# Attention's seven products: signs turned so that weight sums are additions, two of the sums made by accumulating transfers, the second product ahead of the sixth

## The chip, the cores and the metric

One core of one Trainium2 chip runs the whole program. The metric is device time in microseconds (us) of one execution, the median of several. Five engines matter: PE (matrix products, with PEld for its weight loads), DVE (elementwise work), ACT (copies, exponentials, scaled copies), POOL (copies, and the queue of transfers that can add to what lies at their goal), SP (the queue of plain loads).

## The reference

A model of two layers on 512 tokens of width 1024. Layer one is attention with three groups of heads (windows 128, 512, 2048 at dilations 1, 4, 16), then a gated feed-forward part; layer two is an mLSTM mixer and a second feed-forward part. The change lies in the projections of the attention:

```python
proj = (xn @ w_in).reshape(B, S, N_GROUPS, 3, ATTN_HEADS, ATTN_HEAD_DIM)   # w_in: 1024 x 9216
for g, (window, dilation) in enumerate(DIL_CONFIGS):
    q = apply_partial_rope(proj[:, :, g, 0], positions) * scale
    k = apply_partial_rope(proj[:, :, g, 1], positions)
    v = proj[:, :, g, 2]
    o, lse = dilated_window_attention(q, k, v, window, dilation)
    ...
```

All is float32. A product is made of three matmuls on split operands: each operand is a high part (rounded to the format that PE multiplies) and a low part (the rest), and high by high, high by low, low by high are added.

## The kernel before, in words

**Units.** Heads are taken in four pairs (`pr` 0 to 3) and three groups (`g` 0 to 2). A unit `a<pr>g<g>` makes q and k of two heads in one group: two blocks of 256 columns of `w_in`, for 512 tokens. In eleven units (all but `a0g0`) this 2 x 2 block product (weights halved by rows into W1., W2. and by q and k into W.1, W.2; tokens halved) is done with seven products instead of eight, by Winograd's form of Strassen's method. `QK_ORDER` holds the order of the products. Each is 24 matmuls of 128x256 (`qk_unit`, L1100).

**Weights of a unit.** `load_part` (L969) puts the load of one quarter, W11, W12, W22 or W21 (512 KB), on SP's queue. `prepare_part` makes the weight operand of one product. Sums are made in place by DVE (L979):

- P5: W11 becomes W12 - W11
- P6: W11 becomes W22 - that
- P7: W12 becomes W22 - W12
- P4: W21 becomes W21 - W11 (by now P6's operand); made once P2, which uses the plain W21, has been split, in unit a1g2 with P7

Then `split_chunk` makes the high part on ACT (L239) and the low part on DVE (L241). After P2 the next unit's W11 is loaded into the place of this one's, after P7 its W12, after P3 and P4 its W22 and W21. `Feed` prepares two to four products ahead of the one that PE works on.

**Banks of a unit.** P1 goes to bank C11. ACT copies C11 to bank U (L1078, `fill_u`). P2 adds to C11, which is then q of the first half of tokens. P6 adds to U, and ACT copies U to `vu[:, 1]` (L1041). P7 adds to U; DVE adds `vu[:, 0]` (P5's bank, copied by L1038), and this is k of the second half. P3 adds to P5's bank, DVE adds `vu[:, 1]`: k of the first half. P4 adds to U: q of the second half. P7 and P3 end in L1061, P2 and P4 in L1021 (`pack`) and L1055.

**Token sums.** `sum_of` makes S1 to S4 from four blocks of the normalized input (L1272) once, and they serve all units.

**Values.** Two more units, `v0` and `v1` (`values_phase`), make the values of some groups by the same seven products, with sums by DVE (`prepare_values`, L1319); there the order already has P2 ahead of P6.

**Order of the work.** The scores, exponentials and values of the pair before run between the products. `defer` and `advance` place them by ticks: a tick passes after the products at places 1, 3, 5 and 6 (from 0) of a unit in pairs 1 to 3. `run` keeps a block of matmuls together. On POOL's queue lie the copies of the rope's result (L649, L644), stores of the transposed exponentials to DRAM (L897) and loads of them (L902) that wait for those stores. When the program is built, a scheduler puts the instructions of every engine in one order, by their place in the program and by when it expects their operands; on the chip each engine keeps to that order. `behind_scores`, `behind_factors` and `tc.issue_after` give it further constraints.

Accumulating transfers of other parts of the kernel, from which the prediction takes rows: `f1T` (feed-forward output weights, from DRAM, L1887), `oraws` (mLSTM output weights, from DRAM, L2406), `f0T1l` (from SBUF, L1602).

Of the kernel before, what the change touches and what calls it, by code (L numbers as in the profile page):

```python
# [14 lines left out]
AF = mybir.ActivationFunctionType  # L15
ALU = mybir.AluOpType
AX = mybir.AxisListType
P = 128
# [58 lines left out]
def tile_hybrid_dilated_attn_mlstm(  # L77
# [350 lines left out]
    with ExitStack() as actx:  # L428
# [517 lines left out]
        behind_u = []  # L946
        postponed, behind_seventh, held_maxima, copied, differences = [], [], [], [None], [None, None]

        QK_ORDER = ("P1", "P5", "P6", "P2", "P7", "P3", "P4")
        four_k = lambda t: t.rearrange("p (k n) -> p k n", k=4)  # L950
        parts_of = {}

        def by_products(pr, g):
            return g > 0 or pr >= PRODUCTS_FROM

        def load_part(pr, g, key):
            if g > 2:
                pr, g = pr + 1, 0
            if pr == HEADS // 2:
                return  # L960
            if (pr, g, key) == (1, 0, "W11"):
                t = ap.tile([P, 1024], F32, tag="rot", name="a1g0W11")
            elif pr == 0 and key == "W11":
                t = place(("w1", "s1")[g - 1], "a0g%dW11" % g, (P, 1024))
            else:
                pool_, tag, bufs = (ap2, "wa", 1) if key == "W11" else (wp, "wraw", W_BUFS)
                t = pool_.tile([P, 1024], F32, tag=tag, name="a%dg%d%s" % (pr, g, key), bufs=bufs)
            k0, c0 = (int(key[1]) - 1) * 4 * P, g * 3 * D + (int(key[2]) - 1) * D + pr * 256
            nc.sync.dma_start(four_k(t), w_in[k0:k0 + 4 * P, c0:c0 + 256].rearrange("(k p) n -> p k n", p=P))  # L969
            parts_of.setdefault((pr, g), {})[key] = t  # L970

        sixth = [None]
# [1 line left out]
        def prepare_part(pr, g, name):  # L974
            b = parts_of[pr, g]

            def less(out, x, y):
                with behind_scores():
                    nc.vector.tensor_tensor(b[out], b[x], b[y], op=ALU.subtract)  # L979
            src = {"P1": "W11", "P5": "W11", "P6": "W11", "P2": "W21", "P7": "W12", "P3": "W22", "P4": "W21"}[name]  # L980
            if name == "P5":
                less("W11", "W12", "W11")
                differences[0] = last_on(DVE)
            elif name == "P6":
                less("W11", "W22", "W11")
            elif name == "P7":
                with tc.issue_after(sixth[0]) if (pr, g) in ((1, 2), (2, 0)) else nullcontext():
                    less("W12", "W22", "W12")
            with tc.issue_after(differences[1]) if pr and g and name == "P2" else nullcontext():
                whl = split_chunk((b[src], 1024, four_k, "a%dg%d%s" % (pr, g, name)), NARROW)  # L990
            if name == "P6":
                differences[1] = last_on(ACT)
                if (pr, g) in ((1, 2), (2, 0)):
                    sixth[0] = last_on(DVE)
            if (pr, g, name) == (1, 2, "P7"):
                with tc.issue_after(last_on(DVE)):
                    less("W21", "W21", "W11")
            if name == "P5" and not late[0]:
                sixth[0] = last_on(DVE)
            follows = g < 2 or (pr and by_products(pr + 1, 0))  # L1000
            if name == "P2":
                if (pr, g) != (1, 2):
                    less("W21", "W21", "W11")
                if follows:
                    load_part(pr, g + 1, "W11")
            elif name == "P7" and follows:
                load_part(pr, g + 1, "W12")
            elif name in ("P3", "P4") and follows:
                load_part(pr, g + 1, src)
            return whl  # L1010

        def qk_unit(pr, g, qk, then=None):
# [4 lines left out]
            acc = {}  # L1017
            rot = vu = None

            def pack(q, src):  # L1020
                nc.scalar.activation(two_m(rot[0][quarter(q)]), src, AF.Copy)  # L1021

            def each(out, src, th, fn):

# [8 lines left out]
            def finish(name):  # L1033
                nonlocal rot, vu
                if name == "P5":
                    vu = ap.tile([P, 2, SEQ], F32, tag="vu", name=nm + "vu")
                    with behind_factors() if g == 0 else nullcontext():
                        nc.scalar.activation(vu[:, 0], acc["p5"], AF.Copy)  # L1038
                    ahead_of_casts[0] = last_on(ACT)
                elif name == "P6":  # L1040
                    nc.scalar.activation(vu[:, 1], acc["u"], AF.Copy)  # L1041
                    ahead_of_casts[0] = last_on(ACT)
                    if g == 1:
                        copied[0] = last_on(ACT)
                elif name in ("P2", "P4"):
                    th = int(name == "P4")
                    src = acc[target[name]]
                    if th == 0:
                        if g == 0:
                            rot = [npl.tile([P, SEQ], F32, tag=tag, name="rot") for tag in ("rbc", "ssum")]  # L1050
                        else:
                            t = ap.tile([P, 2, SEQ], F32, tag="rot", name="rot")
                            rot = t[:, 0], t[:, 1]
                    pack(th, two_m(src[:R]))
                    each(qk[0], [src], th, lambda to, x: nc.scalar.activation(to, x, AF.Copy))  # L1055
                    ahead_of_casts[0] = last_on(ACT)
                elif name in ("P7", "P3"):
                    th = int(name == "P7")
                    with behind_scores():
                        each(qk[1], [acc[target[name]], vu[:, 1 - th]], th,  # L1060
                             lambda to, x, y: nc.vector.tensor_tensor(to, x, y, op=ALU.add))  # L1061
                    if g == 2:
                        ahead_of_splits[0] = last_on(DVE)
                    if g:
                        pack(2 + th, halves(qk[1], th)[:R])
                    else:
                        for m in range(2):
                            nc.scalar.activation(packed(rot, 2 + th, m, True), turned(qk, 2 + th, m, True), AF.Copy)
                    if g == 2:
                        ahead_of_casts[0] = last_on(ACT)  # L1070
# [191 lines left out]
        def sum_of(name):  # L1262
            nonlocal heads_s
            if name == "S1":
                heads_s = ap.tile([P, 4, 4, HALF], F32R, tag="heads", name="S12")
                sums["chain"] = place("w4", "Sr", (P, 4, HALF))
            raw = place("w5", "S3r", (P, 4, HALF)) if name == "S3" else sums["chain"]
            of = lambda t, kh: lambda i, ks: xblock(t, kh, i)
            chain = lambda i, ks: raw[:, ks]
            x, y, op = {"S1": (of(1, 0), of(1, 1), ALU.add), "S2": (chain, of(0, 0), ALU.subtract),  # L1270
                        "S3": (of(0, 0), of(1, 0), ALU.subtract), "S4": (of(0, 1), chain, ALU.subtract)}[name]
            two(lambda i, ks: nc.vector.tensor_tensor(raw[:, ks], x(i, ks), y(i, ks), op=op))  # L1272
            split_sum(name, raw)

        def first_values():
# [39 lines left out]
        def prepare_values(u, name, hf):  # L1315
            b = {key: t for (key, i), t in blocks[u].items() if i == hf}

            def less(out, x, y):
                nc.vector.tensor_tensor(b[out], b[x], b[y], op=ALU.subtract)  # L1319
            src = {"P1": "W11", "P5": "W11", "P6": "W11", "P2": "W21", "P7": "W12", "P3": "W22", "P4": "W21"}[name]  # L1320
            if name == "P5":
                less("W11", "W12", "W11")
            elif name == "P6":
                less("W11", "W22", "W11")
            elif name == "P7":
                less("W12", "W22", "W12")
            elif name == "P4":
                less("W21", "W21", "W11")
            whl = split_chunk((b[src], 1024, two_k, "v%d%s_%d" % (u, name, hf)))
            following = {"P1": "W11", "P7": "W12", "P3": "W22", "P4": "W21"}.get(name)  # L1330
            if following is not None:
                load_block(u + 1, following, hf)
            if u == len(UNITS) - 1 and hf == 1:
                for key in {"P2": ("W11",), "P6": ("W12", "W22"), "P3": ("W21",)}.get(name, ()):
                    load_part(1, 0, key)
            return whl
# [9 lines left out]
        def values_phase():  # L1346
# [8 lines left out]

            def add(to, src):
                for m in range(2):
                    nc.vector.tensor_tensor(to[:, m], src[m], to[:, m], op=ALU.add)

            def stored(u, tile_, half, n):  # L1360
                nc.gpsimd.dma_start(vD[UNITS[u][n]][half * HALF:(half + 1) * HALF].rearrange("(m p) f -> p m f", p=P), tile_)
# [1466 lines left out]
```

## Time and profile before

| what | value |
|---|---|
| median of three runs | 1342.1 us (1341.83 to 1342.5) |
| profiled execution | 1342.11 us, span of the program in it 1340.3 us |
| granted TensorE clock | 0.999 |
| 57 to 400 us: PE idle, as the list of waits gives it | 4.1 us in nine waits |
| products of the seven-product units | 24 matmuls, 0.11 us from start to start |
| a sum of a quarter on DVE (L979) | 1.2 to 1.3 us, 44 of them |
| high part on ACT, low part on DVE | 1.05 us, 1.22 us |

A row of the timeline has start, duration, engine, line, operation, what it writes and from what, shapes and count; in brackets the idle time before it and what ended it. A row of the list of waits reads: who, for whom, total us, times, longest. A group has its count, busy us, mean ns of one, and the idle time before. In names, `a2g2u` is bank U of unit a2g2, `c` and `p` its banks C11 and P5, `a2g2W` its quarters of weights, `a2g2P_h` and `P_l` a product's high and low part, `S`, `S3`, `S4` the token sums, `xa` the input. `PEld` is a weight load. A landing is counted from issue to arrival.

### The profile page before, as it was taken

To read this page: it belongs to the slowest core of one execution; us is meant where nothing else is said; L and a number is where in the kernel's file an instruction comes from. 1 tells how busy PE (TensorE), PEld (TensorE's weight loads), DVE (VectorE), ACT (ScalarE), POOL (GpSimd) and SP (SyncE) were. 2 spreads that over 40 slices of the span, in tenths; PEclk is the share of its full clock that TensorE was granted. 3 is DMA by queue.
4 is the path that set the end of the run, shared out by engine and by line. 5 is a ranking of instruction groups with operands and counts; after the bars stand their busy time and mean duration, and the time that the engine had idled before them with its cause. 6 is when DMAs were issued, how large, how long until landed. Compare 5 with 4: busy or idle time off the path is not lost. (4 is left out here: it accounts for less than half of the span.)

```text
span 1340.3 us, 23696 instructions
## 1 busy us (share of the span) xinstructions
PE 1323.3 (99%) x9244; PEld 1221.1 (91%) x9244; DVE 1146.4 (86%) x1804; ACT 823.1 (61%) x1313; POOL 214.7 (16%) x292
## 2 busy tenths in 40 slices
PE   9999999999999999999999999999999999999997
PEld 7898899999998889999999998888897999999886
DVE  7988789898876399888888899898889988987887
ACT  6676577677674355554587464795565655559855
POOL 3000014141412001000010110123330211112113
PEclk9999999999999999999999999999999999999999
DMA  9354244556586357334362743326684635447864
GB/s 306 128 181 155 82 142 137 178 152 191 158 288 200 131 146 178 108 110 127 126 161 77 173 138 94 103 64 173 132 168 131 155 108 166 142 142 176 185 173 103
DMA packets 146809, 200.71 MB, mean 150 GB/s; under 512 B 9316, under 2 KB 111524, under 8 KB 146696
## 3 DMA queue, kind: packets, MB, share of 16 engines
q1 hardware_dynamic: 120128, 140.73, 33.4%
q0 software_dynamic: 25344, 58.25, 18.9%
q8 instruction: 73, 1.20, 0.4%
q10 hardware_dynamic: 1224, 0.21, 0.1%
q14 instruction: 40, 0.33, 0.1%
HBM read 172.02 MB, written 22.54 MB: 145 GB/s over the span
## 5 line engine op out<-in xcount | busy, mean ns | idle before, releaser
L1863 POOL DMA_DIRECT2D f0S<-in_ffn_w_out_dram x10 | 8.8, 876 | 246.7 <-DVE f0hid L1782 162.6
L2617 POOL DMA_DIRECT2D hD<-hB x32 | 20.8, 656 | 111.2 <-DVE hB L2614 111.1
L1887 POOL DMA_DIRECT2D f1T<-in_ffn_w_out_dram x15 | 17.8, 1185 | 86.6 <-ACT f1T L1890 26.1
L276 PE MATMUL mo<-n_h,mo_k_h 128*128 128x512 f32 x64 | 25.4, 396 | 0.0
L276 PE MATMUL f1j<-n_h,f1j_l 128*128 128x512 f32 x64 | 25.1, 392 | 0.2 <-DVE f1j_l L241 0.2
L276 PE MATMUL mo<-n_l,mo_k_h 128*128 128x512 f32 x64 | 25.2, 394 | 0.0
L276 PE MATMUL mo<-n_h,mo_k_l 128*128 128x512 f32 x64 | 25.2, 393 | 0.0
L276 PE MATMUL awo<-ao_h,awo_k_h 128*128 128x512 f32 x64 | 25.2, 393 | 0.0
L276 PE MATMUL mqk<-n_h,mqk_k_h 128*128 128x512 f32 x64 | 25.1, 392 | 0.0
L276 PE MATMUL mqk<-n_l,mqk_k_h 128*128 128x512 f32 x64 | 25.1, 392 | 0.0
L276 PE MATMUL f0j<-n_h,f0j_h 128*128 128x512 f32 x64 | 25.0, 391 | 0.0
L276 PE MATMUL f1j<-n_h,f1j_h 128*128 128x512 f32 x64 | 25.0, 391 | 0.0
L276 PE MATMUL awo<-ao_h,awo_k_l 128*128 128x512 f32 x64 | 25.0, 391 | 0.0
L276 PE MATMUL mqk<-n_h,mqk_k_l 128*128 128x512 f32 x64 | 25.0, 390 | 0.0
L241 DVE TENSOR_TENSOR v1P_l<-v1W,v1P_h 128x1024 fp32r<-128x1024 f32 x14 | 17.1, 1223 | 9.2 <-ACT v1P_h L239 9.1
L276 PE MATMUL awo<-ao_l,awo_k_h 128*128 128x512 f32 x64 | 25.0, 390 | 0.0
L276 PE MATMUL f1j<-n_l,f1j_h 128*128 128x512 f32 x64 | 24.9, 390 | 0.0
L276 PE MATMUL f0j<-n_h,f0j_l 128*128 128x512 f32 x64 | 24.9, 390 | 0.0
L276 PE MATMUL f0j<-n_l,f0j_h 128*128 128x512 f32 x64 | 24.9, 389 | 0.0
L241 DVE TENSOR_TENSOR v0P_l<-v0W,v0P_h 128x1024 fp32r<-128x1024 f32 x14 | 17.0, 1221 | 6.9 <-ACT v0P_h L239 6.9
L239 ACT ACTIVATE v1P_h<-v1W 128x1024 fp32r<-128x1024 f32 x14 | 14.8, 1058 | 12.8 <-PE v1u L1398 4.0
L1890 ACT ACTIVATE f1T<-f1T 128x1024 f32<-128x1024 f32 x15 | 15.8, 1053 | 8.9 <-DVE f1P_2w_l L241 3.1
(2812 smaller groups left out, 6106.4 us busy)
## 6 DMA issues: line engine op xcount, KB each, us to landing
f0j_w<-in_ffn_w_in_dram SPq DMA_DIRECT2D x17, 512.0 KB, 5.3
f1j_w<-in_ffn_w_in_dram SPq DMA_DIRECT2D x17, 512.0 KB, 6.7
f1T<-in_ffn_w_out_dram POOLq DMA_DIRECT2D x15, 512.0 KB, 6.7
f0hid<-in_ffn_w_in_dram SPq DMA_DIRECT2D x9, 512.0 KB, 5.2
f1hid<-in_ffn_w_in_dram SPq DMA_DIRECT2D x9, 512.0 KB, 5.3
v0W<-in_attn_w_in_dram SPq DMA_DIRECT2D x8, 512.0 KB, 6.2
v1W<-in_attn_w_in_dram SPq DMA_DIRECT2D x8, 512.0 KB, 4.0
awo_k_w<-in_attn_w_out_dram SPq DMA_DIRECT2D x8, 512.0 KB, 4.2
```

Source lines behind the costliest of these rows:

```text
L239: nc.scalar.activation(hi[:, :n], raw[:, :n], AF.Copy)
L241: nc.vector.tensor_tensor(lo[:, :n], raw[:, :n], hi[:, :n].bitcast(F32), op=ALU.subtract)
L276: nc.tensor.matmul(acc, whl[a][:, k, m * P:(m + 1) * P], pairs[b][kk], start=(kk == 0 and (a, b) == SPLITS[0]), stop=(kk == nk - 1 and (a, ...
L1863: nc.gpsimd.dma_start(t, src[1][:, ks], accum_op=ALU.add)
L1887: nc.gpsimd.dma_start(view(to), weight_rows(hk * UNITS + u, n), accum_op=ALU.add)
L1890: nc.scalar.activation(x, x, AF.Copy, scale=-1.0)
L2617: nc.gpsimd.dma_start(hD[k // 4].rearrange("(b i) x -> i b x", i=R)[:, :, c0:c0 + R], t[R * a_:R * (a_ + 1)])
```

## The change

The signs of the method are turned so that every sum of weights is an addition; the token sums S1, S2, S4 and the results change sign to make up for it (a scale of -1 in ACT's copies of q, `scalar_tensor_tensor` with -1 where DVE subtracted or added).

In the eleven units of q and k:

- P5's and P6's sums stay on DVE, as additions.
- P7's sum is made by a transfer on POOL's queue, issued with P5: W12 (no longer needed plain once P5's sum has read it) gets W22 added from DRAM.
- P4's sum is made by a transfer on POOL's queue, issued with P6: W21 gets W11 added, SBUF to SBUF. It has to wait for P6's sum and for P2's split.
- P2 is done ahead of P6. P6's split is to follow P2's on ACT (before: P2's followed P6's).
- The next unit's W11 is loaded after P6, and has to wait until P4's transfer has read this one's.
- Two constraints on P7's difference in units a1g2 and a2g0 fall away.

In the value units the sums stay on DVE.

```diff
-        QK_ORDER = ("P1", "P5", "P6", "P2", "P7", "P3", "P4")
+        QK_ORDER = ("P1", "P5", "P2", "P6", "P7", "P3", "P4")
...
+        def weights_part(pr, g, key):
+            k0, c0 = (int(key[1]) - 1) * 4 * P, g * 3 * D + (int(key[2]) - 1) * D + pr * 256
+            return w_in[k0:k0 + 4 * P, c0:c0 + 256].rearrange("(k p) n -> p k n", p=P)
...
-            def less(out, x, y):
+            def total(out, x, y):
                 with behind_scores():
-                    nc.vector.tensor_tensor(b[out], b[x], b[y], op=ALU.subtract)
+                    nc.vector.tensor_tensor(b[out], b[x], b[y], op=ALU.add)
             src = {"P1": "W11", "P5": "W11", "P6": "W11", "P2": "W21", "P7": "W12", "P3": "W22", "P4": "W21"}[name]
             if name == "P5":
-                less("W11", "W12", "W11")
+                total("W11", "W12", "W11")
                 differences[0] = last_on(DVE)
+                nc.gpsimd.dma_start(four_k(b["W12"]), weights_part(pr, g, "W22"), accum_op=ALU.add)
             elif name == "P6":
-                less("W11", "W22", "W11")
-            elif name == "P7":
-                with tc.issue_after(sixth[0]) if (pr, g) in ((1, 2), (2, 0)) else nullcontext():
-                    less("W12", "W22", "W12")
-            with tc.issue_after(differences[1]) if pr and g and name == "P2" else nullcontext():
+                total("W11", "W22", "W11")
+            with tc.issue_after(differences[1]) if pr and g and name == "P6" else nullcontext():
                 whl = split_chunk((b[src], 1024, four_k, "a%dg%d%s" % (pr, g, name)), NARROW)
-            if name == "P6":
+            if name == "P2":
                 differences[1] = last_on(ACT)
                 if (pr, g) in ((1, 2), (2, 0)):
                     sixth[0] = last_on(DVE)
-            if (pr, g, name) == (1, 2, "P7"):
-                with tc.issue_after(last_on(DVE)):
-                    less("W21", "W21", "W11")
+            if name == "P6":
+                nc.gpsimd.dma_start(b["W21"], b["W11"], accum_op=ALU.add)
...
-            if name == "P2":
-                if (pr, g) != (1, 2):
-                    less("W21", "W21", "W11")
+            if name == "P6":
                 if follows:
                     load_part(pr, g + 1, "W11")
...
-            def pack(q, src):
-                nc.scalar.activation(two_m(rot[0][quarter(q)]), src, AF.Copy)
+            def pack(q, src, scale=1.0):
+                nc.scalar.activation(two_m(rot[0][quarter(q)]), src, AF.Copy, scale=scale)
...
-                    pack(th, two_m(src[:R]))
-                    each(qk[0], [src], th, lambda to, x: nc.scalar.activation(to, x, AF.Copy))
+                    pack(th, two_m(src[:R]), -1.0)
+                    each(qk[0], [src], th, lambda to, x: nc.scalar.activation(to, x, AF.Copy, scale=-1.0))
...
-            x, y, op = {"S1": (of(1, 0), of(1, 1), ALU.add), "S2": (chain, of(0, 0), ALU.subtract),
-                        "S3": (of(0, 0), of(1, 0), ALU.subtract), "S4": (of(0, 1), chain, ALU.subtract)}[name]
-            two(lambda i, ks: nc.vector.tensor_tensor(raw[:, ks], x(i, ks), y(i, ks), op=op))
+            x, y, both = {"S1": (of(1, 1), of(1, 0), False), "S2": (chain, of(0, 0), True),
+                          "S3": (of(0, 0), of(1, 0), False), "S4": (of(0, 1), chain, True)}[name]
...
+                if both:
+                    nc.vector.scalar_tensor_tensor(raw[:, ks], x(i, ks), -1.0, y(i, ks), op0=ALU.mult, op1=ALU.subtract)
...
-                    nc.vector.tensor_tensor(to[:, m], src[m], to[:, m], op=ALU.add)
+                    nc.vector.scalar_tensor_tensor(to[:, m], src[m], -1.0, to[:, m], op0=ALU.mult, op1=ALU.subtract)
```

More of the change, by code (lines that the diff above doesn't have):

```diff
@@ L967, in load_part @@
                 t = pool_.tile([P, 1024], F32, tag=tag, name="a%dg%d%s" % (pr, g, key), bufs=bufs)
-            k0, c0 = (int(key[1]) - 1) * 4 * P, g * 3 * D + (int(key[2]) - 1) * D + pr * 256
-            nc.sync.dma_start(four_k(t), w_in[k0:k0 + 4 * P, c0:c0 + 256].rearrange("(k p) n -> p k n", p=P))
+            nc.sync.dma_start(four_k(t), weights_part(pr, g, key))
             parts_of.setdefault((pr, g), {})[key] = t
@@ L1269, in sum_of, with combine @@
             chain = lambda i, ks: raw[:, ks]
-            x, y, op = {"S1": (of(1, 0), of(1, 1), ALU.add), "S2": (chain, of(0, 0), ALU.subtract),
-                        "S3": (of(0, 0), of(1, 0), ALU.subtract), "S4": (of(0, 1), chain, ALU.subtract)}[name]
-            two(lambda i, ks: nc.vector.tensor_tensor(raw[:, ks], x(i, ks), y(i, ks), op=op))
+            x, y, both = {"S1": (of(1, 1), of(1, 0), False), "S2": (chain, of(0, 0), True),
+                          "S3": (of(0, 0), of(1, 0), False), "S4": (of(0, 1), chain, True)}[name]
+            def combine(i, ks):
+                if both:
+                    nc.vector.scalar_tensor_tensor(raw[:, ks], x(i, ks), -1.0, y(i, ks), op0=ALU.mult, op1=ALU.subtract)
+                else:
+                    nc.vector.tensor_tensor(raw[:, ks], x(i, ks), y(i, ks), op=ALU.subtract)
+            two(combine)
             split_sum(name, raw)
@@ L1316, in prepare_values, with total @@
             b = {key: t for (key, i), t in blocks[u].items() if i == hf}
-            def less(out, x, y):
-                nc.vector.tensor_tensor(b[out], b[x], b[y], op=ALU.subtract)
+            def total(out, x, y):
+                nc.vector.tensor_tensor(b[out], b[x], b[y], op=ALU.add)
             src = {"P1": "W11", "P5": "W11", "P6": "W11", "P2": "W21", "P7": "W12", "P3": "W22", "P4": "W21"}[name]
             if name == "P5":
-                less("W11", "W12", "W11")
+                total("W11", "W12", "W11")
             elif name == "P6":
-                less("W11", "W22", "W11")
+                total("W11", "W22", "W11")
             elif name == "P7":
-                less("W12", "W22", "W12")
+                total("W12", "W22", "W12")
             elif name == "P4":
-                less("W21", "W21", "W11")
+                total("W21", "W21", "W11")
             whl = split_chunk((b[src], 1024, two_k, "v%d%s_%d" % (u, name, hf)))
```

## The prediction

> **What bounds the kernel now.** I read the page first, then who waited for whom on PE in the stretch that the change touches (57 to 400 us), then PE's rows in order of time around the longest wait.
>
> ```profile
> PE 1323.3 (99%) x9244; PEld 1221.1 (91%) x9244; DVE 1146.4 (86%) x1804; ACT 823.1 (61%) x1313; POOL 214.7 (16%) x292
> ```
>
> PE is busy for 1323.3 us of a span of 1340.3. The change keeps every matmul, so what it can give is PE's waiting in the seven-product units. The list of waits shows how little that is:
>
> ```profile
> PE a1g2u L1100 <- DVE a1g2P_l L241: 1.3, 1, 1.3
> PE a2g2u L1100 <- DVE a2g2P_l L241: 0.6, 1, 0.6
> PE a3g2u L1100 <- DVE a3g2P_l L241: 0.5, 1, 0.5
> ...
> PE a1g2c L1100 <- ACT a1g2P_h L239: 0.3, 1, 0.3
> PE a0g1u L1100 <- DVE a0g1P_l L241: 0.3, 1, 0.3
> PE a0g2u L1100 <- DVE a0g2P_l L241: 0.3, 1, 0.3
> ```
>
> Six waits, 3.3 us together: five for the low part of a weight half (DVE, L241), one for a high part. All are in P6 or P2 but a0g1's, which is in P7. PE loses more than the idle time, since a matmul's modelled end runs past the next one's start. The worst place, unit a1g2:
>
> ```profile
> 223.76 0.28 PE L1100 MATMUL a1g2p<-S,a1g2P_l 128*128 128x256 f32 x1
> 223.87 0.39 PE L1100 MATMUL a1g2u<-S,a1g2P_h 128*128 128x256 f32 x2
> 224.60 0.38 PE L1100 MATMUL a1g2c<-xa_h,a1g2P_h 128*128 128x256 f32 x1 [0.34 <-ACT a1g2P_h L239]
> 224.83 0.28 PE L1100 MATMUL a1g2c<-xa_l,a1g2P_h 128*128 128x256 f32 x1
> 226.37 0.39 PE L1100 MATMUL a1g2u<-S,a1g2P_l 128*128 128x256 f32 x1 [1.27 <-DVE a1g2P_l L241]
> 226.60 0.40 PE L1100 MATMUL a1g2u<-S,a1g2P_h 128*128 128x256 f32 x2
> ```
>
> Undisturbed, matmuls start 0.11 us apart (223.76, 223.87). Here 224.83 is followed by 226.37 and that by 226.60: 1.43 + 0.12 = 1.55 us lost where 1.27 are listed, 0.28 on top of the wait. So the six cost 3.3 + 6 x 0.28 = 5.0 us, 0.37% of the run: the ceiling of the gain. The rows show a second thing: two matmuls of P2 (a1g2c) stand inside P6 (a1g2u). PE's queue is not in the order of the products; work that was expected to be ready had been put ahead.
>
> **The change part by part.**
>
> *Two of four sums leave DVE.* Eleven units with four sums each; the costliest and the cheapest group:
>
> ```profile
> L979 DVE TENSOR_TENSOR a1g2W<-a1g2W,a1g2W 128x1024 f32<-128x1024 f32 x4 | 5.3, 1320 | 0.0
> L979 DVE TENSOR_TENSOR a0g1W<-a0g1W,a0g1W 128x1024 f32<-128x1024 f32 x4 | 4.8, 1209 | 0.0
> ```
>
> 22 instructions at 1.2 to 1.3 us are 27 us of DVE, none of it on PE's path by itself: it counts where a low part is queued behind a sum.
>
> *P2 ahead of P6.* P2 needs no sum, and P6's split gets 24 matmuls x 0.11 = 2.7 us more, beyond any of these waits. Only in a1g2 does more stand before it: the rope on DVE, from the shuffle to the last addition.
>
> ```profile
> 222.38 0.75 DVE L630 STREAM_SHUFFLE rot<-rot 128x512 f32<-128x512 f32 x1
> 224.49 0.69 DVE L639 TENSOR_TENSOR rot<-rot 128x512 f32<-128x512 f32 x1
> ```
>
> With P2's low part (1.2 us) put ahead of the rope, the rope ends at 225.2 + 1.2 = 226.4 and P6's low part at 227.6; P6's third matmul is then due at 224.1 + 2.7 = 226.8. Between 0 (low part ahead of the rope) and 0.8 us I take 0.4. a0g1's P7 now has its sum from a transfer begun two products earlier than its subtraction was. Back come 5.0 - 0.4 = 4.6 us.
>
> *P7 directly behind P6.* Both add into the bank U, which L1041 copies in between. Until now P2 stood there. The last matmul of P6, and the copy:
>
> ```profile
> 207.44 0.28 PE L1100 MATMUL a1g1u<-S,a1g1P_l 128*128 128x256 f32 x1
> 207.81 0.60 ACT L1041 ACTIVATE a1g1vu<-a1g1u 128x512 f32<-128x512 f32 x1 [1.12 <-PE a1g1u L1100]
> 301.47 0.28 PE L1100 MATMUL a2g2u<-S,a2g2P_l 128*128 128x256 f32 x1
> 303.77 0.57 ACT L1041 ACTIVATE a2g2vu<-a2g2u 128x512 f32<-128x512 f32 x1
> 304.40 0.39 PE L1100 MATMUL a2g2u<-S3h,a2g2P_h 128*128 128x256 f32 x1
> ```
>
> A prompt copy ends 208.41 - 207.44 = 0.97 us after P6's last matmul began, and PE follows a copy by 304.40 - 304.34 = 0.06. P7 starts 1.03 instead of 0.11 us later: 0.92, with the slow next matmul 1.04 us a unit. In a2g2, where ACT had other copies first, it would be 2.93 - 0.11 = 2.8. In the three g0 units the deferred scores or values stand between the fourth product and P7 and cover it, as here:
>
> ```profile
> 187.38 0.27 PE L806 MATMUL a0s<-a0g_k,a0g_q 128*128 128x128 f32 x1
> 190.87 0.37 PE L1100 MATMUL a1g0u<-S3h,a1g0P_h 128*128 128x256 f32 x1
> ```
>
> Eight units are left. Lower bound 0: P3 adds into another bank, and eight of its matmuls ahead of P7 (8 x 0.11) fill the gap, as P2's two did in a1g2. Upper bound 8 x 1.04 = 8.3 us, some 12 with a2g2 and a3g2 at 2.8. P3 can go ahead where its low part is there; of a2g1 and of a0g1:
>
> ```profile
> 282.46 1.19 DVE L241 TENSOR_TENSOR a2g1P_l<-a2g1W,a2g1P_h 128x1024 fp32r<-128x1024 f32 x1
> 284.44 0.28 PE L1100 MATMUL a2g1u<-S3h,a2g1P_h 128*128 128x256 f32 x1
> 69.66 1.23 DVE L241 TENSOR_TENSOR a0g1P_l<-a0g1W,a0g1P_h 128x1024 fp32r<-128x1024 f32 x1
> 68.22 0.39 PE L1100 MATMUL a0g1u<-S3h,a0g1P_h 128*128 128x256 f32 x1
> ```
>
> In a2g1 P3's low part ended 0.8 us before P7 began, and DVE now has two sums fewer; in a0g1 it began 1.4 us after. So I let the six units of pairs 1 to 3 pay nothing and the two of pair 0 pay 1.0 each: 2.0 us.
>
> *The 22 transfers.* Nearest rows: half-megabyte accumulating transfers from DRAM, and the one transfer of tile f0T1l, SBUF to SBUF (last row, issue to landing):
>
> ```profile
> f1T<-in_ffn_w_out_dram POOLq DMA_DIRECT2D x15, 512.0 KB, 6.7
> oraws<-in_mlstm_w_out_dram POOLq DMA_DIRECT2D x6, 512.0 KB, 7.7
> ...
> DMA to landing us min/median/max: 7.3/7.3/7.3
> ```
>
> The tight places are the g2 units, where POOL waits for other transfers. Of a2g2: P5's sum, POOL's blocked load, how long a load of the next unit's weights (a3g0W) took to land, and that unit's first product:
>
> ```profile
> 289.27 1.23 DVE L979 TENSOR_TENSOR a2g2W<-a2g2W,a2g2W 128x1024 f32<-128x1024 f32 x1
> 299.58 0.56 POOL L902 DMA_DIRECT2D a1pT<-a1pD  x1 [4.51 <-DMA a1pD<-a1pB]
> DMA to landing us min/median/max: 4.1/4.1/4.1
> 315.76 0.28 PE L1100 MATMUL a3g0c<-xa_h,a3g0P_h 128*128 128x256 f32 x1
> ```
>
> P7's transfer: 290.5 + 7.7 + split 2.3 (ACT 1.05, DVE 1.22) = 300.5 against P7 at 304.4, 3.9 us to spare. P4's, if it is stuck behind the blocked load: 300.1 + 7.3 = 307.4. Only then may SP reload W11, which DVE used to free at once: 307.4 + 4.1 + 2.3 = 313.8 against 315.76, 2.0 us to spare. So on these rows it fits; since every spare is near a transfer's own spread, I take 0.5 us in all, bounds 0 and the price of the third rival below.
>
> A page of the Trainium skill, "DMA: Bandwidth & Descriptors" (section "Anatomy of one DMA — SWDGE (gpsimd) path"), puts such a transfer at 2.0 us plus its bytes over 436 GB/s, 3.2 us here as an estimate from that page. The rows above show 6.7 to 7.7 for accumulating ones and decide; by the page's figure the 0.5 us would be 0.
>
> *Edits at nothing.* Signs in `scalar_tensor_tensor` instead of `tensor_tensor`, and as scale of an ACT copy: the first pair of rows has 680 against 683 ns, and ACT multiplies by its scale in the same pass. Subtractions turned to additions keep their length.
>
> ```profile
> L2502 DVE SCALAR_TENSOR_TENSOR y<-og,y 128x512 f32<-128x512 f32 x8 | 5.4, 680 | 0.0
> L1358 DVE TENSOR_TENSOR v1v<-v1u,v1v 128x512 f32<-128x512 f32 x2 | 1.3, 683 | 0.0
> ```
>
> *Sum.* -4.6 + 2.0 + 0.5 = -2.1, and at the two other ends -5.0 and +8.3 or more. The profiled execution took 1342.1 us, the median of the runs: 1340.0.
>
> **The rivals.** *First: the copy of U is hidden everywhere, pair 0 too*, because DVE without the sums has P3's low part early. -4.6 + 0.5 = -4.1: 1338.0. For it: P2's two matmuls inside P6. Against it: a0g1's row, 1.4 us late.
>
> *Second, the other side: P7 waits for the copy in all eight units.* Place: between P6 and P7. Price: 1.04 each, -4.6 + 8.3 + 0.5 = +4.2: 1346.3, more if ACT is late as in a2g2. It decides from five units on (4.6 / 1.04 is 4.4). For it: the dependence is new and ACT's copy cannot be shorter than 0.57. Against it: the order on PE was seen to step around a wait.
>
> *Third: a transfer goes behind POOL's long work.* In a1g1 POOL copied for nine microseconds:
>
> ```profile
> L649 POOL COPY a1g_q<-rot x4: 1353/1417/1476, 203.5 to 207.7; 32x256 f32<-32x256 f32 x4
> L649 POOL COPY a1g_k<-rot x4: 391/846/1447, 209.1 to 212.2; 32x256 f32<-32x256 f32 x4
> ```
>
> Issued at 212.6 it lands at 219.9, while the same unit's P4 began at 215.7: 4.2 + 2.3 = 6.5 us in this one unit; 1340.0 + 6.5 = 1346.5. Issued ahead of the copies it costs nothing, in the middle some 2: 1342. The skill's page "SBUF — State Buffer" (section "Who interferes with whom") speaks against the change here: a DVE operation with two SBUF inputs blocks a GpSimd operation that reads SBUF. That agrees with copies of one shape that take 391 to 1476 ns in the two rows above.
>
> **How the numbers follow.** My case (some of the gain paid back at U, -0.5 to -4): 0.45, forecast 1340.0, own range 1338 to 1341.6. First rival 0.2, second 0.18, third 0.17. A change under 0.2%, 2.7 us, can hardly be told from none. Faster by more: all of the first and two fifths of my case, 0.38. Slower by more: the second and half of the third, 0.26. The rest, 0.36, is the same. The range 1337 to 1346.5 leaves out the far ends of the first and second rival.
>
> **What would show it.** Right: no wait of `a2g2u` or `a3g2u` for L241; two rows of L979 a unit; P3's matmuls (`p` from `S4`) between P6 and P7. Wrong: PE or PEld waiting for L1041 in the g1 and g2 units; ACT waiting in L239 for a transfer into `W`; the next unit's `c` late behind W11. A gain beyond 5 us would mean that PE lost time in these units that the list of waits does not show.

## The result, and the profile after

The changed kernel takes 1375.4 us (median; 1374.7 to 1377.2) against 1342.3 in the same comparison: ratio 1.0247, 95% interval 1.0235 to 1.0259, 33 us slower. The forecast was 1340.0, its range ended at 1346.5. Below, ratios to the kernel before are also given in microseconds of 1342.3, since before was measured anew beside each group of runs (its medians went from 1342.3 to 1343.7).

The first line of the page of after, same columns as in the prediction:

```profile
PE 1335.6 (97%) x9244; PEld 1232.0 (90%) x9244; DVE 1123.5 (82%) x1782; ACT 823.2 (60%) x1313; POOL 233.2 (17%) x314
```

DVE lost 22.9 us of work and 22 instructions, as the change says. PE has the same 9244 matmuls and is busy for 12.3 us longer; the span grew by 32.6 us (1340.3 to 1372.9), so PE's idle time grew by 20.3. Both parts need a reason. The list of waits on PE in the units of the change (who, for whom, total us, times, longest):

```profile
PE a1g1u L1098 <- ACT a1g1vu L1039: 6.0, 1, 6.0
PE a2g1u L1098 <- ACT a2g1vu L1039: 3.6, 1, 3.6
PE a3g1u L1098 <- ACT a3g1vu L1039: 3.5, 1, 3.5
PE a2g0c L1098 <- ACT a2g0P_h L239: 3.1, 1, 3.1
PE a2s L806 <- POOL a2g_k L644: 2.3, 1, 2.3
...
PE a2g2c L1098 <- DVE a2g2P_l L241: 0.6, 1, 0.6
...
PE a1g2c L1098 <- DVE a1g2P_l L241: 0.5, 1, 0.5
```

(L1098, L1039 and L1053 of after are L1100, L1041 and L1055 of before.) Three long waits are for U's copy, all in g1 units; before had none of them. The old waits of P6 for a low part are gone, but P2 (`c`) now waits for its own: 0.6 us in a2g2 and 0.5 in a1g2, two of the same three units.

Why is U's copy late? The timeline around a1g1, all engines in order of time:

```profile
203.28 3.41 POOL L649 COPY a1g_q<-rot 32x256 f32<-32x256 f32 x4 [5.01 <-DVE a0cf L863]
206.75 3.41 POOL L649 COPY a1g_k<-rot 32x256 f32<-32x256 f32 x4
210.11 0.90 POOL L997 DMA_DIRECT2D a1g1W<-a1g1W  x1
210.50 0.28 PE L1098 MATMUL a1g1u<-S,a1g1P_l 128*128 128x256 f32 x1
211.18 0.28 PE L1098 MATMUL a1g1p<-S4h,a1g1P_l 128*128 128x256 f32 x1
215.84 1.06 ACT L239 ACTIVATE a1g1P_h<-a1g1W 128x1024 fp32r<-128x1024 f32 x1 [6.67 <-DMA a1g1W<-a1g1W]
216.80 0.58 ACT L1039 ACTIVATE a1g1vu<-a1g1u 128x512 f32<-128x512 f32 x1
217.43 0.58 PE L1098 MATMUL a1g1u<-S3h,a1g1P_h 128*128 128x256 f32 x1 [5.97 <-ACT a1g1vu L1039]
217.81 0.42 PE L1098 MATMUL a1g1u<-S3l,a1g1P_h 128*128 128x256 f32 x1
```

Read it from the bottom. P7 starts at 217.43 because U's copy ended then. The copy could have run from 210.8 on, when P6's last matmul (210.50) was through, but ACT stood for 6.67 us in the high part of *P4* (L239), which is ahead of the copy on ACT's queue and waits for the transfer into W21. That transfer was issued at 210.11, right behind POOL's eight copies of the rope, and landed 5.6 us later. PE did what the prediction foresaw: it took six matmuls of P3 (`p`, to 211.18) to fill the gap. Then it had nothing left.

The last row shows where most of the other 12.3 us lie: its matmul takes 0.42 us instead of 0.28, and from there on they start 0.21 us apart instead of 0.11. The stretch 200 to 220 us of after (busy us and count of PE, PEld, DVE, ACT, POOL, then granted clock, DMA share, GB/s) has a clock of 0.89; that of before has 1.00:

```profile
200.00:220.00 20.00, 14.03 (x113) 13.83 (x113) 13.32 (x30) 9.33 (x15) 7.57 (x9) 0.89 0.51 125
```

In five stretches, which begin during or soon after the first five waits of the list, the clock is 0.50. The first of them, and the sum of all five:

```profile
215.57:222.38 6.81, 4.95 (x23) 4.95 (x24) 1.22 (x1) 4.56 (x9) 0.00 (x0) 0.50 0.71 232
sum 23.82, PE 20.53 PEld 20.24 DVE 10.06 ACT 14.07 POOL 2.75; mean PE 4.11 PEld 4.05 DVE 2.01 ACT 2.81 POOL 0.55
```

PE is busy for 20.5 us in them. At half the clock half of that, 10.3 us, is extra: an estimate, which leaves 2.0 of the 12.3 us to other causes.

The fourth wait of the list starts from the same transfer, by another way (SPq is the queue of plain loads):

```profile
237.71 0.92 POOL L997 DMA_DIRECT2D a1g2W<-a1g2W  x1
244.61 0.37 SPq L972 DMA_DIRECT2D a2g0W<-in_attn_w_in_dram  x1
250.66 0.28 PE L1098 MATMUL a1g2u<-xa_h,a1g2P_l 128*128 128x256 f32 x1
252.97 1.06 ACT L239 ACTIVATE a2g0P_h<-a2g0W 128x1024 fp32r<-128x1024 f32 x1 [5.99 <-DMA a2g0W<-in_attn_w_in_dram]
254.08 0.58 PE L1098 MATMUL a2g0c<-xa_h,a2g0P_h 128*128 128x256 f32 x1 [3.15 <-ACT a2g0P_h L239]
```

W21's transfer lands 6.9 us after its issue; only then may SP load the next unit's W11 into the place that it read (244.61). That load took 8.4 us, and a2g0's first product starts 3.4 us after a1g2's last matmul (250.66). From 240 to 252 us the 16 DMA engines were busy throughout (a share of 0.96 to 1.09 in each slice of 4 us, as the profile counts it), with other loads for this unit among their work; whether the load would have been quicker without them was not tried.

**Theory A:** the loss is the transfer into W21. It stands behind other work on POOL's queue, and its late landing holds what is queued behind P4's high part on ACT, and the next W11 on SP. **Rival B:** it is the order: P7, directly behind P6, must wait for U's copy. **Rival C:** it is the seventh product's transfer from DRAM.

### The profile page after: what moved, and what is told of

Its sections match the earlier page's. It is cut to its first block, busy times and chain, and to the rows that moved or that the text cites. A ratio compares the mean times of both kernels' runs of the same rounds, so it can differ in the third digit from the quotient of the medians.

```text
span 1372.9 us, 23741 instructions
## 1 busy us (share of the span) xinstructions
PE 1335.6 (97%) x9244; PEld 1232.0 (90%) x9244; DVE 1123.5 (82%) x1782; ACT 823.2 (60%) x1313; POOL 233.2 (17%) x314
## 5 line engine op out<-in xcount | busy, mean ns | idle before, releaser
L241 DVE TENSOR_TENSOR v1P_l<-v1W,v1P_h 128x1024 fp32r<-128x1024 f32 x14 | 17.1, 1223 | 9.3 <-ACT v1P_h L239 9.3
L241 DVE TENSOR_TENSOR v0P_l<-v0W,v0P_h 128x1024 fp32r<-128x1024 f32 x14 | 17.0, 1222 | 6.8 <-ACT v0P_h L239 6.8
L239 ACT ACTIVATE v1P_h<-v1W 128x1024 fp32r<-128x1024 f32 x14 | 14.8, 1058 | 12.5 <-PE v1u L1402 4.0
```

The source lines that it names most:

```text
L239: nc.scalar.activation(hi[:, :n], raw[:, :n], AF.Copy)
L241: nc.vector.tensor_tensor(lo[:, :n], raw[:, :n], hi[:, :n].bitcast(F32), op=ALU.subtract)
```

## The experiments

| run | what it is | ratio to before, 95% interval | us |
|---|---|---|---|
| after | the change | 1.0247 (1.0235 to 1.0259) | +33.2 |
| e1 | P4's sum on DVE | 1.0076 (1.0059 to 1.0093) | +10.2 |
| e2 | P7's sum on DVE | 1.0258 (1.0243 to 1.0274) | +34.6 |
| e3 | both on DVE (new order, signs) | 1.0075 (1.0058 to 1.0091) | +10.1 |
| e4 | both transfers, old order | 1.0294 (1.0279 to 1.0310) | +39.5 |
| e5 | U's copy ahead of P4's high part | 1.0208 (1.0193 to 1.0224) | +27.9 |
| e6 | POOL's copies behind the transfer | 1.0154 (1.0138 to 1.0169) | +20.7 |
| e7 | signs only | 0.9997 (0.9987 to 1.0006) | -0.4 |
| e9 | signs, P7's transfer, old order | 0.9987 (0.9977 to 0.9996) | -1.7 |
| e10 | signs, new order in g2 units only | 1.0033 (1.0023 to 1.0044) | +4.4 |
| e11 | signs, new order in pair 0 only | 1.0012 (1.0002 to 1.0021) | +1.6 |
| e12 | P4's sum on DVE in g1 units | 1.0106 (1.0091 to 1.0121) | +14.2 |
| e13 | P4's sum on DVE in g2 units | 1.0196 (1.0180 to 1.0211) | +26.3 |

**e1, e2, e3: which sum.** e1:

```diff
-                nc.gpsimd.dma_start(b["W21"], b["W11"], accum_op=ALU.add)
+                total("W21", "W21", "W11")
```

> The fourth product's sum back on DVE; the seventh's stays a transfer, the order of the products stays. Theory A (the transfer into W21 stands behind POOL's copies, and its late landing holds ACT's queue with U's copy in it, and the next unit's W11): the waits of 6.0, 3.6 and 3.5 us for L1039 in the three g1 units fall under 0.7 us each, the 3.1 us for a2g0's first product and the 2.3 us for a2's scores go too, and so do the stretches of halved clock: 1343 us, 1340 to 1347. Rival B (the seventh product directly behind the sixth must wait for U's copy whatever the transfers do): the three waits stay above 1 us each and more units show them; 1347 to 1365. Rival C (the seventh product's transfer, 512 KB from DRAM, is what is late): above 1365.

e2, and e3 with both edits:

```diff
-                nc.gpsimd.dma_start(four_k(b["W12"]), weights_part(pr, g, "W22"), accum_op=ALU.add)
...
+            elif name == "P7":
+                total("W12", "W22", "W12")
```

> The seventh product's sum back on DVE; the fourth's stays a transfer, the order stays. Theory A (the transfer into W21): nothing of the loss goes, 1370 to 1378 us, and P7 in a1g1 still waits some 6 us for L1039. Rival B (U's copy by itself): the same time as after, but then the run with the fourth sum on DVE must be slow too. Rival C (the seventh product's transfer): 1340 to 1350.

> Both sums back on DVE: what is left of the change is the order (second product ahead of the sixth) and the signs. Theory A: no loss is left but what U's copy costs by itself, which the prediction put at 0 to 8.3 us against 4.6 us gained: 1338 to 1346, and within 2 us of the run with only the fourth sum on DVE. Rival B: P7 waits about 1 us for L1039 in eight units, or more where P4's high part stands ahead of the copy on ACT: 1346 or more.

Measured: 1354.3, 1378.2 and 1353.3 us. P4's transfer is 33.2 - 10.2 = 23 us of the loss; taking P7's transfer away gains nothing (e2, +34.6), so rival C falls. But e1 and e3 missed their ranges: some 10 us stay with no transfer into W21, so theory A is not the whole. What e3 still waits for:

```profile
PE a3s L786 <- DVE a3own L740: 2.5, 1, 2.5
PE a0g1p L1099 <- ACT a0g1P_h L239: 1.4, 1, 1.4
PE a2s L806 <- POOL a2g_k L644: 1.1, 1, 1.1
...
PE a1g2u L1099 <- ACT a1g2vu L1040: 0.5, 1, 0.5
PE a0g1u L1099 <- ACT a0g1vu L1040: 0.5, 1, 0.5
```

Hardly any of it is U's copy (two waits of 0.5), so rival B in its first form falls too; e10 and e11 below take these rows up.

**e7, e9: signs and the other transfer alone.** e7 is before with the signs of after; e9 is e7 with the sum of P7 by transfer:

```diff
+                nc.gpsimd.dma_start(four_k(b["W12"]), weights_part(pr, g, "W22"), accum_op=ALU.add)
...
-            elif name == "P7":
-                with tc.issue_after(sixth[0]) if (pr, g) in ((1, 2), (2, 0)) else nullcontext():
-                    total("W12", "W22", "W12")
```

> Only the signs of the change: order and sums on DVE as in before, the sums as additions, the scale of -1 in ACT's copies and scalar_tensor_tensor where DVE added or subtracted. All theories: nothing, within 1.5 us of before (1341.5 to 1344.5). If the signs have a price after all, part of the 9 us of the run with both sums on DVE is theirs.

> The signs, and only the seventh product's sum by a transfer; the order and the fourth product's sum as in before. It takes 11 sums of 1.2 us off DVE and puts no wait on W21 or W11. If the relief of DVE is worth what the prediction said: the waits of a1g2, a2g2 and a3g2 for a low part shrink and the time is 1338 to 1341. If they are not set by these sums: 1342 to 1344. If the transfer for the seventh product has a price of its own: above 1345.

Measured: 1342.25, no change; and 1340.86, 0.13% faster than before (interval 0.04 to 0.23%). This is the one version of this study that beats both kernels, by less than the 0.2% that the prediction called measurable, though the interval leaves out 1. So the order costs 10.1 + 0.4 = 10.5 us and P7's transfer is worth about 1.3. Of e9's waits:

```profile
PE a1g2u L1101 <- DVE a1g2P_l L241: 1.1, 1, 1.1
...
PE a2g2u L1101 <- DVE a2g2P_l L241: 0.5, 1, 0.5
PE a3g2u L1101 <- DVE a3g2P_l L241: 0.5, 1, 0.5
```

With eleven sums fewer on DVE, P6's three waits for a low part are 1.1, 0.5 and 0.5 us instead of 1.3, 0.6 and 0.5: those sums were not the main thing that stood ahead of the low parts.

**e5, e6: the place on ACT's queue, and that on POOL's.** P4's high part got ahead of U's copy because `Feed` is filled to four products at the third place of the order. That place was P6 (so P4 was prepared after U's copy); now it is P2. e5 prepares P4 after P6 in the g1 units:

```diff
-                copy_first = name == "P6" and (pr, g) == (1, 2)
+                copy_first = name == "P6" and pr > 0 and (g == 1 or (pr, g) == (1, 2))
...
-                    feed.fill(feed.ahead + ((pr, g, n) != (1, 2, 1)))
+                    feed.fill(feed.ahead + ((pr, g, n) != (1, 2, 1) and (g, n) != (1, 2)))
```

> Both transfers as in after, but in the g1 units of pairs 1 to 3 the fourth product is prepared only once the sixth is finished, so that on ACT's queue U's copy (L1039) stands ahead of the fourth product's high part (L239). Theory A, in which the place on ACT's queue turns a late transfer into a stall of the seventh product: its waits in a1g1, a2g1, a3g1 fall from 6.0, 3.6, 3.5 us to under 0.7; P7 and P3 fill 4 us, a1g1's P4 then waits 1 to 2 us, the others none. Saved 6.6 + 5.5 + 5.6 with the halved clock behind each stall: 1357.8 us, 1354 to 1363. Rival D (the late transfer costs the same wherever PE meets it): the wait moves from P7 to P4 with its length, 1370 to 1377.

Measured: 1371.8, 5.3 us less than after where theory A had 17.6. ACT's rows in a1g1 and the waits on PE:

```profile
211.13 0.60 ACT L1039 ACTIVATE a1g1vu<-a1g1u 128x512 f32<-128x512 f32 x1 [1.71 <-PE a1g1u L1098]
215.06 1.07 ACT L239 ACTIVATE a1g1P_h<-a1g1W 128x1024 fp32r<-128x1024 f32 x1 [3.32 <-DMA a1g1W<-a1g1W]
218.61 1.06 ACT L239 ACTIVATE a1g2P_h<-a1g2W 128x1024 fp32r<-128x1024 f32 x1 [2.49 <-DMA a1g2W<-in_attn_w_in_dram]
```

```profile
PE a2g2p L1098 <- ACT a2g_q L1053: 2.0, 1, 2.0
...
PE a1g2p L1098 <- ACT a1g_q L1053: 1.8, 1, 1.8
...
PE a1g1u L1098 <- DVE a1g_k L1059: 1.3, 1, 1.3
```

U's copy is prompt (211.13) and no g1 unit of pairs 1 to 3 waits for it any more, as foreseen. But ACT still stands for W21 (3.32 us) and then for the next unit's W11 (2.49), its other work falls behind, and P5 of the *next* unit (`p`, a3g2's too) waits 1.8 to 2.0 us for the copy of q that frees its bank. The number is rival D's, but the place is one that neither theory named: a queue that has stood is late for what follows on it.

e6 leaves ACT alone and moves POOL's copies behind the transfer:

```diff
-                        defer(1, lambda: back(True))
+                        defer(2, lambda: back(True))
```

> As after, but POOL's eight copies of the rope (L649) are deferred by one tick more, so that in a2g1 and a3g1 the transfer into W21 stands ahead of all eight on POOL's queue, and in a1g1 ahead of the last two. Theory A (the transfer is late because of POOL's queue): the waits for L1039 of 3.6 and 3.5 us in a2g1 and a3g1 go with the halved clock behind them (2 x 5.4 us), a1g1's 6.0 falls by 1.7: 1363 us, 1359 to 1367. Rival E (the transfer is late because its operands are late or because it lands slowly): 1372 to 1377, and the waits stay.

Measured: 1363.4, 0.4 us from the number expected. POOL in a2g1, and the first of the waits on PE:

```profile
287.49 0.96 POOL L997 DMA_DIRECT2D a2g1W<-a2g1W  x1
...
290.52 3.43 POOL L649 COPY a2g_q<-rot 32x256 f32<-32x256 f32 x4 [1.29 <-DVE a1cf L863]
```

```profile
PE a1g1u L1098 <- ACT a1g1vu L1039: 5.1, 1, 5.1
PE a2g0c L1098 <- ACT a2g0P_h L239: 2.9, 1, 2.9
```

The waits of a2g1 and a3g1 for L1039 are gone from the list, with ACT's order as in after. In a1g1 six of the eight copies still stand ahead of the transfer, and its wait only falls from 6.0 to 5.1, by half of the 1.7 us expected; that the total agrees to 0.4 us is in part luck. So what has to be moved is the transfer's issue.

**e4: the old order with both transfers.** P6 ahead of P2 again; the transfer into W21 follows P2's split.

```diff
-        QK_ORDER = ("P1", "P5", "P2", "P6", "P7", "P3", "P4")
+        QK_ORDER = ("P1", "P5", "P6", "P2", "P7", "P3", "P4")
```

> Both transfers kept, but the sixth product ahead of the second again, as in before; on ACT U's copy now stands ahead of the fourth product's high part. The two runs without transfers say that the order alone costs some 9 us and the transfer into W21 some 22. If the two add: 1344 + 20 = 1364 us, 1356 to 1372, with ACT waiting in L239 for W21 and the next unit's W11 late as in after. If the transfer only hurts because the new order lets ACT's queue put the fourth product's high part ahead of U's copy: P7's three waits go and the time is 1343 to 1352.

Measured: 1382.5, above every value named. Against e9, the same kernel without the transfer into W21, it costs 39.5 + 1.7 = 41 us, more than in the new order. ACT's and DVE's rows in a1g1, and PE's waits:

```profile
216.02 1.06 ACT L239 ACTIVATE a1g1P_h<-a1g1W 128x1024 fp32r<-128x1024 f32 x1 [8.37 <-DMA a1g1W<-a1g1W]
217.11 1.22 DVE L241 TENSOR_TENSOR a1g1P_l<-a1g1W,a1g1P_h 128x1024 fp32r<-128x1024 f32 x1 [5.19 <-ACT a1g1P_h L239]
218.25 0.68 DVE L1059 TENSOR_TENSOR a1g_k<-a1g1u,a1g1vu 128x512 f32<-128x512 f32 x1
```

```profile
PE a1g1u L1098 <- DVE a1g_k L1059: 4.0, 1, 4.0
PE a2g1u L1098 <- DVE a2g_k L1059: 3.8, 1, 3.8
```

U's copy is ahead on ACT, and now the work is held up on DVE: P7's k (L1059) is queued behind P4's low part, and P4 may not add to U before k is read. The wait has moved from P7 to P4. Why the whole is dearer than in the new order was not taken apart.

**e12, e13: in which units.** As after, with P4's sum on DVE where the condition holds:

```diff
-                nc.gpsimd.dma_start(b["W21"], b["W11"], accum_op=ALU.add)
+                if g == 1:      # e13: g == 2
+                    total("W21", "W21", "W11")
+                else:
+                    nc.gpsimd.dma_start(b["W21"], b["W11"], accum_op=ALU.add)
```

> As after, but the fourth product's sum on DVE in the g1 units, where POOL copies the rope; a transfer in the g0 and g2 units. Theory A: P7's waits for L1039 in a1g1, a2g1, a3g1 go with the halved clock behind them (8.5 + 5.3 + 5.3), the late W11 in front of a2g0 and a3g0 stays, and 2 to 3 us come back at a3's scores as in the run with this sum on DVE everywhere: 1359 us, 1355 to 1364. If the late transfer costs as much through W11 as through ACT: 1364 or more.

> As after, but the fourth product's sum on DVE in the g2 units, where the next unit's W11 was late; a transfer in the g0 and g1 units. Theory A: the waits in a2g0 (3.1 and 0.5 us, with halved clock behind them 6.3), in a3g0 (0.8 and 0.9) and part of the 2.3 at a2's scores go, the three in the g1 units stay: 1366 us, 1362 to 1370. If W11 is late for another reason than W21's transfer, 1373 to 1377.

Measured: 1357.3 and 1369.5, both inside their ranges. The g1 units are worth 33.2 - 14.2 = 19.0 us, the g2 units 6.9; together 25.9 against 23.0 for all. The longest wait left in e12 is the next unit's W11, while U's copy holds no g1 unit any more:

```profile
PE a2g0c L1101 <- ACT a2g0P_h L239: 2.9, 1, 2.9
```

In e13 it is the other way round, 6.3 us in a1g1 for U's copy and none for W11.

**e10, e11: where the order costs.** The order is chosen by unit, all sums on DVE:

```diff
+        def turned_order(pr, g):
+            return pr > 0 and g == 2      # e11: pr == 0
+
+        def qk_order(pr, g):
+            return ("P1", "P5") + (("P2", "P6") if turned_order(pr, g) else ("P6", "P2")) + ("P7", "P3", "P4")
```

> All sums on DVE, signs turned, and the second product ahead of the sixth only in a1g2, a2g2 and a3g2; everywhere else the old order. Theory O (with the sixth product second, U's copy and what ACT and DVE have queued behind it come one product, 24 x 0.11 = 2.7 us, closer to the unit's end, where the scores wait for it): the run with the new order everywhere showed in these units and behind them 0.7 us more at a2's scores, 2.6 at a3's, 0.9 each in a2g2 and a3g2, and 0.5 less in a1g2: 1342.3 + 4.6 = 1347 us, 1345 to 1350. Rival P (the order costs in every unit alike, 11 us over eleven units): 1345 with no wait at a3's scores. Rival N (it costs where the attention of the pair before does not cover U's copy, that is in pair 0): 1342 to 1343.

> All sums on DVE, signs turned, the second product ahead of the sixth only in a0g1 and a0g2, where the prediction had put 1.0 us each. The run with the new order everywhere showed 1.56 + 0.66 us of stalls in a0g1 and 0.85 in a0g2 against 0.45 and 0.44 before, 2.2 us more: 1344.5, 1343.5 to 1346. If the copy of U is the whole price of the order (rival N): 1350 or more. If pair 0 pays nothing: 1342.3.

Measured: +4.4 us (expected 4.6) and +1.6 (expected 2.2); rival N falls by both runs. Rival P falls by the wait at a3's scores, which it excluded; by the time alone it was close (+2.7 us named for e10, +3.1 to +5.9 measured). The wait at a3's scores in e10, two rows of DVE and one of PE, and below the two of before:

```profile
381.10 2.17 DVE L894 STREAM_TRANSPOSE a2pB<-a2p 128x1920 f32<-128x1920 f32 x1
392.82 0.29 DVE L740 CUSTOM_DVE_ANT_0 a3p<-a3s,acst 128x128 f32<-128x128 f32 x1 [4.74 <-DMA a2pD<-a2pB]
393.59 1.16 PE L786 MATMUL a3s<-a3g_k,a3g_q 128*128 128x128 f32 x8 [2.96 <-DVE a3own L740]
```

```profile
377.22 2.17 DVE L894 STREAM_TRANSPOSE a2pB<-a2p 128x1920 f32<-128x1920 f32 x1
388.27 0.29 DVE L740 CUSTOM_DVE_ANT_0 a3p<-a3s,acst 128x128 f32<-128x128 f32 x1 [0.90 <-DMA a2pD<-a2pB]
```

DVE's maxima need a place that the store of the transposed exponentials frees. The transposition (L894) comes 3.9 us later than before and the maxima that wait for its store 4.6 us, while PE reached these scores only 1.1 us later (389.58 against 388.46); the difference is its wait. On DVE's queue of e10 it stands behind P4's low part; that and the link to U's copy one product nearer to the unit's end were read from the rows and not tried by themselves. 10.5 - 4.4 - 1.6 = 4.5 us of the order, in the g0 and g1 units of pairs 1 to 3 or in how the parts act together, were not tried alone, and part of these numbers may be the clock (see the last section).

## Why the prediction was wrong, step by step

- **The 22 transfers** (taken at 0.5 us, measured at 23 for W21's and -1.4 to +0.1 for W12's). This step failed. Its landing times were about right (W21's took 4.5 to 6.9 us, W12's 5.8 to 9.1, against 6.7 to 7.7 taken). It looked for the tight place in the g2 units and left POOL's copies in a1g1 to the third rival, which had the cause right and the effect too small: one unit where there are three, and P4's own lateness (6.5 us) as the price. It did not ask what is queued on ACT *behind the instruction that waits for the transfer*. The row for that was in the prediction: ACT's U copy at 207.81 in a1g1, with P4's start 8 us off. As soon as P4's high part is prepared one product earlier, the copy stands behind it.
- **The next W11** (2.0 us to spare, worked out for a3g0): failed. The load was taken at 4.1 us; it took 8.4 in front of a2g0. In front of a3g0 it was issued at 326.2, and the high part that waits for it started at 335.6, 9.4 us later; a3g0's first product then waits 0.8 us.
- **P7 behind P6, U's copy** (2.0 us in pair 0, nothing elsewhere): the size was about right, the wait was mostly another. e11 measures 1.6 us, but there PE took P3 ahead of P7 and waited 1.5 us in a0g1 and 0.7 in a0g2 for P3's high part; for U's copy it waited 0.5. That the sizes agree is luck in part. In pairs 1 to 3, e3 waits 0.5 us for the copy in one unit, and a2g0, one of the g0 units that were held to be covered, waits 0.6 in after. And it put nothing on what the new order shifts behind the copy, as far as the transposition in e10.
- **P2 ahead of P6, and sums off DVE** (4.6 us back): wrong. P2's own low part is the late one now (0.5 to 0.6 us in after, 1.8 in a1g2 of e10), and the eleven sums that left DVE in e9 gave 1.3 us.
- **Signs free**: right, 0.9997 (0.9987 to 1.0006).
- **What would show it**: all three signs of being wrong came, PE waiting for L1041 (here L1039) in g1 units, ACT waiting in L239 for a transfer, the next unit's `c` late behind W11. So did the three signs of being right (no wait of `a2g2u` or `a3g2u` for L241, two rows of sums a unit, P3's matmuls between P6 and P7): those could not tell the two cases apart.
- **Not in the sum at all**: the granted clock, some 10 of the 12.3 us by which PE's busy time grew.

## What to carry to other kernels

When a sum goes from an engine to a transfer, price both queues: what the issue stands behind (here POOL's copies), and what stands behind the first instruction that waits for the landing (here U's copy on ACT, k on DVE). A list that prepares work by its place in an order, and not by its name, changes every in-order queue when two entries swap. Undoing the order on one queue only moved the wait (e5); issuing the transfer earlier removed it in the two units where it went ahead of all the copies (e6).

## What the runs showed of the hardware

**A stall on PE is at times followed by a halved clock.** The stalls of 6.0, 3.1, 3.6 and 3.5 us in after are each followed by 16 to 22 matmuls 0.21 us apart instead of 0.11. Shorter ones can do it too. In e11 two stalls of 1.45 and 0.50 us, both within 2.5 us, were followed by a clock of 0.50 from 70.1 to 73.5 us (PE's rows):

```profile
69.22 0.39 PE L1108 MATMUL a0g1p<-S4h,a0g1P_h 128*128 128x256 f32 x1 [1.45 <-ACT a0g1P_h L239]
69.45 0.28 PE L1108 MATMUL a0g1p<-S4l,a0g1P_h 128*128 128x256 f32 x1
70.22 0.58 PE L1108 MATMUL a0g1u<-S3h,a0g1P_h 128*128 128x256 f32 x1 [0.50 <-ACT a0g1vu L1049]
70.60 0.41 PE L1108 MATMUL a0g1u<-S3l,a0g1P_h 128*128 128x256 f32 x1
```

The same two waits in e3 were not followed by it, nor was the single one of 3.2 us at a3's scores in e1. So the price of a stall differs from one run to another. It does between executions of one kernel as well: the four of e3 took 1350.9 and 1351.8 us at a mean clock of 0.999, and 1354.7 twice at 0.996. Some 3 us of what the order costs go with the clock and come in one execution and not in another.

The Trainium skill, "TensorE: Matmul & The Clock Gate" (section "Part 1: The HAM clock gate"), says that the clock is halved after an idle window of about 3.4 us and that the window is free-running. The stalls of 3.5 us and more and the chance element agree, and so do the stretches of clock 0.50 in after, which last 3.4 or 6.8 us. The threshold does not, since a stall of 3.1 us sufficed in after, and 1.45 and 0.50 us in e11.

**POOL's copies, slow and quick.** The copies of q in a1g1 take 854 ns in the median; before they took 1417, quoted in the prediction beside the rule of the Trainium skill's page "SBUF — State Buffer" (section "Who interferes with whom"). That is no sign of the rule: in a2g1 and a3g1 the same copies took 854 and 862 ns already before, and from 203.5 to 207.7 us DVE is busy all the time in both kernels. What made the copies of a1g1 slow in before stays open. It was no help either: the transfer stood behind them all the same.
